# Norm chains whose VectorE steps keep an operand in PSUM, with the adaLN sums held back meanwhile

## The chip, the cores and the metric

The kernel runs on one core of a Trainium2 chip. The metric is the device time of one execution in microseconds (us). TensorE multiplies matrices into PSUM; VectorE, ScalarE and GpSimd work on what lies in SBUF, and the first two of these also on PSUM; SyncE queues the loads. In the profile they are PE (and PEld for its weight loads), DVE, ACT, POOL and SP.

## The reference, cut to what matters

Two layers of a diffusion backbone over 256 latent tokens (`x`) and 256 context tokens (`h`), width 1024. Each sub-layer is preceded by an RMS norm and an adaLN modulation, whose shifts, scales and gates come from a conditioning vector through a large matrix:

```python
def rms_norm(x, g):
    y = xf * lax.rsqrt(jnp.mean(xf * xf, axis=-1, keepdims=True) + RMS_EPS)
    return (y * g).astype(x.dtype)

def modulate(h, shift, scale):
    return h * (1.0 + scale) + shift

for l in range(DEPTH):                       # DEPTH = 2
    sh1, sc1, g1, ..., g3 = split(s_c @ w_mod[l] + b_mod[l], 9)      # and again for the context
    x = x + 0.5 * g1 * swiglu(modulate(rms_norm(x, norm_g[l, 0]), sh1, sc1), ...)
    y, yc = token_mixer(modulate(rms_norm(x, norm_g[l, 1]), sh2, sc2), ...)
    x = x + g2 * y
    x = x + 0.5 * g3 * swiglu(modulate(rms_norm(x, norm_g[l, 2]), sh3, sc3), ...)
```

The context tokens go through the same steps, except that nothing is computed for them behind the mixer of the last layer.

## The kernel before, in words

**Layout.** Activations lie feature-major: `x[k]`, k = 0 to 7, is a tile of 128 features by 512 tokens, of which columns 0 to 255 are the latent tokens (r = 0) and 256 to 511 the context tokens (r = 1). Every fp32 product is made from three TensorE passes over operands split into a rounded part and a rest (`mm3`): `u_hi`, `u_lo` for activations, `w_hi`, `w_lo` for weights. For each weight chunk of 128x1024, ScalarE makes `w_hi` (a cast) and GpSimd makes `w_lo = w_raw - w_hi`, three chunks deep (`SPLIT_BUFS`).

**A norm.** `norm_chain(l, i, r, n)` is a generator for one norm and one half r of the tokens. TensorE sums squares into a PSUM tile `n_ss` (columns 256 and 257). `rsqrt` turns the two sums into 1/sqrt with a bit trick and three Newton rounds, 13 small VectorE steps on the SBUF tiles `rs_v`, `rs_s`, `rs_y`, `rs_a`. `norm_diag` spreads the result over a diagonal matrix `n_diag`, and a matmul with `ones` broadcasts it into columns 0 to 255 of `n_ss`. Then for each k, on 128x256: `n_t = x[k] * A * n_ss` (A is the gain with the adaLN scale), `u_hi = n_t + shift`, `u_lo = n_t + shift - u_hi`. `n_t` is a fresh SBUF tile for each k, and the three steps of successive k are interleaved (n_t of k, u_hi of k-1, u_lo of k-2). With both halves (n > LAT) chain 0 stops after k = 3 until chain 1 has made its first four.

Nine such chains run: both halves for the norms called here (0,1) [layer 0, before the mixer], (0,2) [layer 0, before the second FFN], (1,0) and (1,1), and one for (1,2). The first norm of all, (0,0), has code of its own (`first_tokens`).

**Around it.** A two-half norm is started while TensorE ends the product in front of it (`rest` in `last_down`, or `last_fn`), and is used by `up(..., both=True)` or `proj_f2`: TensorE goes through k = 0 to 3 of r = 0, then of r = 1, with two weight chunks at once, and then through k = 4 to 7 of both with the next two chunks. The second of these needs a weight buffer that the first pass gives back.

**adaLN sums.** Most of the adaLN products are made on VectorE: `mod_gen` adds up `mod_acc = mod_w * scv + mod_acc` over 128x512 tiles, paced at 42 us for two blocks (`MOD_PACE`), as the side "mods". A few blocks are left for TensorE as work within the norms (`norm_fill`, tiles `mod`, `mod_ev`, `mod_t`).

**What sets the order.** Each engine runs its instructions in the order in which the program writes them. `Program.round` resumes all generators in turn (norms, urgent work, sides) after each group of matmuls, and a gated operation is written when a model clock says that its operands are there. A change of any step therefore moves later instructions too. In the profile L196 is the line of all gated operations and L169 of all others, so groups are told apart by their tiles.

Of the kernel before, what the change touches and what calls it, by code (L numbers as in the profile page):

```python
# [11 lines left out]
F32 = mybir.dt.float32  # L12
F32R = mybir.dt.float32r
I32 = mybir.dt.int32
AF = mybir.ActivationFunctionType
ALU = mybir.AluOpType
AX = mybir.AxisListType

P = 128
D = 1024  # L20
KT = D // P
LAT = 256
# [8 lines left out]
EPS = 1e-6  # L31
# [169 lines left out]
class Program:  # L201
# [127 lines left out]
    def round(self):  # L329
        self.wakes = []  # L330
        n = self.clock.count
        self.first = True
        for waiting in (self.norms, self.urgent):
            for g in list(waiting):
                if not self._resume(g):
                    waiting.remove(g)
        self.first = False
        for name in sorted(self.sides, key=lambda name: name == "mods"):
            if name in self.sides:
                self._step(name)  # L340
        return self.clock.count > n
# [91 lines left out]
def tile_backbone(ctx: ExitStack, tc: tile.TileContext, I: dict, out: bass.AP):  # L433
# [4 lines left out]
    sml = ctx.enter_context(tc.tile_pool(name="sml", bufs=4))  # L438
# [7 lines left out]
    prog = Program(nc, rpool, wpool)  # L446
# [3 lines left out]
    gpe, gdve, gact = Gated(prog, "PE", nc.tensor), Gated(prog, "DVE", nc.vector), Gated(prog, "ACT", nc.scalar)  # L450
# [3 lines left out]
    def S(name):  # L454
        return slot.tile([P, 512], F32, name=name, tag="s")
# [60 lines left out]
        yield from gact.copy(r32(hi), src)  # L516
        yield from gdve.tensor_tensor(r32(lo), src, hi, op=ALU.subtract)

    def rsqrt(src, n, scale):

        v = sml.tile([P, 32], F32, name="rs_v", tag="rs_v")[:, :n]
        s = sml.tile([P, 32], F32, name="rs_s", tag="rs_s")[:, :n]
        y = sml.tile([P, 32], F32, name="rs_y", tag="rs_y")[:, :n]
        a = sml.tile([P, 32], F32, name="rs_a", tag="rs_a")[:, :n]
        yield from gdve.tensor_scalar(v, src, scale, EPS, op0=ALU.mult, op1=ALU.add)
        yield from gdve.tensor_scalar(s.bitcast(I32), v.bitcast(I32), 1, None, op0=ALU.logical_shift_right)
        yield from gdve.tensor_scalar(y.bitcast(I32), s.bitcast(I32), -1, 0x5F3759DF, op0=ALU.mult, op1=ALU.add)
        yield from gdve.tensor_scalar(v, v, -0.5, None, op0=ALU.mult)
        for _ in range(3):
            yield from gdve.tensor_tensor(a, y, y, op=ALU.mult)  # L530
            yield from gdve.tensor_tensor(a, a, v, op=ALU.mult)
            yield from gdve.scalar_tensor_tensor(y, a, 1.5, y, op0=ALU.add, op1=ALU.mult)
        return y


    ident = cst.tile([P, P], F32, name="ident")
# [9 lines left out]
    x = [cst.tile([P, NT], F32, name=f"x{k}") for k in range(KT)]  # L546
    scv = cst.tile([P, KT, 32], F32, name="scv")

    st = {"gated": set(), "th": {}}
# [238 lines left out]
    def norm_chain(l, i, r, n):  # L788

        mod = st["mod", l]  # L790
        w = slice(r * LAT, (r + 1) * LAT)
        if r == 0:
            st["A"] = prog.now(norm_scale(l, i, 0, KT))
            st["u"] = [(r32(U("u_hi")), r32(U("u_lo"))) for _ in range(KT)]
            st["done"] = [0, 0]
        yield from prog.banks(1)
        ps = side_bank("n_ss")
        qs = st["sq"]
        for t in range(2):
            c = slice((2 * r + t) * P, (2 * r + t + 1) * P)  # L800
            for j, q in enumerate(qs):
                yield from gmm(ps[:, 256 + t : 257 + t], q[:, c], ones[:, 0:1], j == 0, j == len(qs) - 1)
        rstd = yield from rsqrt(ps[:, 256:258], 2, 1.0 / D)
        dg = yield from norm_diag(rstd, LAT)
        rb = ps[:, :LAT]
        yield from gmm(rb, ones, dg, True, True)
        B = mod[:, 24 * i : 24 * i + 8, :]
        ts = {}
        for step in range(KT + 2):
            k = step  # L810
            if k < KT:
                ts[k] = S("n_t")[:, :LAT]
                yield from gdve.scalar_tensor_tensor(ts[k], x[k][:, w], st["A"][:, k, r : r + 1], rb, op0=ALU.mult, op1=ALU.mult)
            if step == KT - 1:
                prog.release(1)
            k = step - 1
            if 0 <= k < KT:
                hi = st["u"][k][0][:, w]
                yield from gdve.tensor_scalar(hi, ts[k], B[:, k, r : r + 1], None, op0=ALU.add)
            k = step - 2  # L820
            if k >= 0:
                hi, lo = (a[:, w] for a in st["u"][k])
                yield from gdve.scalar_tensor_tensor(lo, ts.pop(k), B[:, k, r : r + 1], hi.bitcast(F32), op0=ALU.add, op1=ALU.subtract)
                st["done"][r] = k + 1
            while r == 0 and n > LAT and k == 3 and st["done"][1] < 4:
                yield None

    def norm_start(l, i, r, n):
        prog.norms.append(norm_chain(l, i, r, n))
# [37 lines left out]
    def norm_diag(rstd, n):  # L867
        nt = n // P
        dg = S("n_diag")[:, :n]
        for t in range(nt):  # L870
            yield from gdve.tensor_scalar(dg[:, t * P : (t + 1) * P], ident, rstd[:, t : t + 1], None, op0=ALU.mult)
        return dg
# [1144 lines left out]
    for l in range(DEPTH):  # L2017
        last = l == DEPTH - 1
        n = LAT if last else NT
# [51 lines left out]
```

## Time and profile before

| | us |
|---|---|
| median of 3 runs | 2881.67 |
| lowest, highest | 2880.91, 2881.89 |
| the profiled execution | 2878.06 |
| its span | 2876.3 |
| TensorE busy in the span | 2777.6 |
| VectorE busy | 1662.6 |
| GpSimd busy | 1288.1 |
| ScalarE busy | 1007.2 |

The span is the time between the first and the last recorded instruction; what is outside it is 1.8 us. An engine counts as busy while an instruction is recorded on it, also while that instruction is held up.

### The profile page before, as it was taken

The numbers are of one execution on the slowest core, as the hardware profiler recorded it, in microseconds if no ns is written. First come the engines' busy times: TensorE is split into PE (matmuls) and PEld (weight loads), VectorE is DVE, ScalarE is ACT, GpSimd is POOL, SyncE is SP. The second block draws the span as 40 slices with busy tenths as digits, with TensorE's granted clock in tenths as the row PEclk, the third lists the DMA queues.
The fourth block names the chain that finished last, engine by engine and source line by source line (L and its number), as shares of the span: only waits on it lengthen the run. The fifth ranks groups of instructions, "written<-read, shape, count | busy, mean of one in ns | idle before, by whom it ended". The sixth has DMA issues, their size and how long they took to land.

```text
span 2876.3 us, 39661 instructions
## 1 busy us (share of the span) xinstructions
PE 2777.6 (97%) x15547; PEld 2330.8 (81%) x15547; DVE 1662.6 (58%) x2970; ACT 1007.2 (35%) x1598; POOL 1288.1 (45%) x585
## 2 busy tenths in 40 slices
PE   8999998999999999999999989999999998999999
PEld 6888877778777888877888878888787777899899
DVE  5654566768765675675545575212555659757522
ACT  2222223433444344322312212222244345454443
POOL 3444433224333442434444434444433455657687
PEclk9999999999999999999999989999999999999999
DMA  6444443224222222433444434333323334435554
GB/s 228 159 147 133 151 129 107 77 81 131 80 73 78 81 74 62 161 125 109 144 143 139 161 102 146 101 96 99 110 70 85 95 100 115 132 103 180 172 184 155
DMA packets 295647, 346.46 MB, mean 120 GB/s; under 512 B 15541, under 2 KB 238806, under 8 KB 295460
## 3 DMA queue, kind: packets, MB, share of 16 engines
q1 hardware_dynamic: 294964, 343.58, 38.0%
q8 instruction: 122, 2.00, 0.3%
q14 instruction: 65, 0.53, 0.1%
q0 software_dynamic: 320, 0.28, 0.0%
q10 hardware_dynamic: 176, 0.07, 0.0%
HBM read 342.83 MB, written 1.05 MB: 120 GB/s over the span
## 4 chain that ended last, share of the span: by engine, by line
PE 86%; DVE 8%; issue 4%; POOL 1%; DMA 0%; ACT 0%; SPq 0%; DVEq 0%; POOLq 0%; ACTq 0%
PE up L169 28%; PE pf L169 17%; PE dn L169 15%; PE pt L169 15%; PE a_s L196 2%; PE a_t L196 2%; PE n_o L196 1%; POOL w_lo L196 1%; PE g_o L196 1%; PE q_o L196 1%; PE g_U L196 1%; PE a_qk L196 1%; DVE rs_a L196 1%; DVE z L169 1%; DVE a_p L196 1%
## 5 line engine op out<-in xcount | busy, mean ns | idle before, releaser
L196 POOL TENSOR_TENSOR w_lo<-w_raw,w_hi 128x1024 fp32r<-128x1024 f32 (+1 forms) x508 | 1228.2, 2422 | 1538.3 <-ACT w_hi L196 1480.3
L196 ACT CAST w_hi<-w_raw 128x1024 fp32r<-128x1024 f32 (+1 forms) x504 | 520.6, 1036 | 993.5 <-issue 311.9
L169 PE MATMUL up<-u_hi,w_lo 128*128 128x512 f32 (+1 forms) x1504 | 534.3, 355 | 16.1 <-POOL w_lo L196 16.0
L169 PE MATMUL up<-u_hi,w_hi 128*128 128x512 f32 (+1 forms) x1504 | 536.5, 357 | 6.4 <-DVE u_hi L196 4.1
L169 PE MATMUL up<-u_lo,w_hi 128*128 128x512 f32 (+1 forms) x1504 | 534.3, 355 | 5.0 <-DVE u_lo L196 4.8
L196 DVE SCALAR_TENSOR_TENSOR mod_acc<-mod_w,scv,mod_acc 128x512 f32<-128x512 f32 x364 | 372.7, 1070 | 57.3 <-DMA mod_w<-w_mod 57.0
L169 PE MATMUL dn<-ff_h,w_hi 128*128 128x512 f32 (+1 forms) x1528 | 396.8, 349 | 0.0
L169 PEld LDWEIGHTS up<-u_hi,w_hi 128*128 128x128 f32 x1504 | 290.9, 193 | 56.0 <-issue 11.0
L169 PEld LDWEIGHTS up<-u_hi,w_lo 128*128 128x128 f32 x1504 | 290.9, 193 | 54.9 <-POOL w_lo L196 17.1
L169 PEld LDWEIGHTS up<-u_lo,w_hi 128*128 128x128 f32 x1504 | 290.7, 193 | 43.4 <-DVE u_lo L196 6.0
L169 PEld LDWEIGHTS dn<-ff_h,w_hi 128*128 128x128 f32 x1528 | 267.6, 189 | 38.9 <-ACT w_hi L196 1.7
L169 PE MATMUL dn<-ff_h,w_lo 128*128 128x512 f32 (+1 forms) x764 | 265.9, 348 | 0.0
L169 PE MATMUL pt<-w_hi,u_hi 128*128 128x512 f32 x640 | 261.8, 409 | 0.0
L169 PE MATMUL pf<-u_hi,w_hi 128*128 128x256 f32 (+1 forms) x736 | 250.9, 341 | 10.3 <-DVE u_hi L196 7.0
L169 PE MATMUL pt<-w_hi,u_lo 128*128 128x512 f32 x640 | 250.8, 392 | 0.0
L169 PE MATMUL pt<-w_lo,u_hi 128*128 128x512 f32 x640 | 250.5, 391 | 0.0
L169 PE MATMUL pf<-u_hi,w_lo 128*128 128x256 f32 (+1 forms) x736 | 239.9, 326 | 8.7 <-POOL w_lo L196 8.7
L169 PE MATMUL pf<-u_lo,w_hi 128*128 128x256 f32 (+1 forms) x736 | 240.3, 327 | 5.8 <-DVE u_lo L196 5.7
L169 DVE TENSOR_TENSOR ff_h<-ff_a,up 128x512 f32<-128x512 f32 (+1 forms) x88 | 53.3, 620 | 317.0 <-PE up L169 278.7
L169 PE MATMUL pf<-y,w_hi 128*128 128x512 f32 (+1 forms) x768 | 195.6, 345 | 3.1 <-DVE y L196 1.9
L169 PEld LDWEIGHTS pf<-u_hi,w_hi 128*128 128x128 f32 x736 | 143.7, 195 | 30.9 <-issue 9.4
L169 DVE SCALAR_TENSOR_TENSOR x<-dn,ff_g,x 128x256 f32<-128x256 f32 x112 | 47.1, 478 | 202.0 <-PE dn L169 201.8
(227 smaller groups left out, 4043.0 us busy)
## 6 DMA issues: line engine op xcount, KB each, us to landing
w_raw<-ffn_w_in SPq DMA_DIRECT2D x176, 512.0 KB
w_raw<-w_in SPq DMA_DIRECT2D x168, 512.0 KB
mod_w<-w_mod SPq DMA_DIRECT2D x288, 256.0 KB
w_raw<-ffn_w_out SPq DMA_DIRECT2D x80, 512.0 KB
w_raw<-w_branch SPq DMA_DIRECT2D x48, 512.0 KB
w_raw<-w_out SPq DMA_DIRECT2D x16, 512.0 KB
w_raw<-ffn_w_out SPq DMA_DIRECT2D x16, 256.0 KB
n_rel<-nat_rpb SPq DMA_DIRECT2D x32, 109.5 KB
```

The costliest lines, as they stand in the source:

```text
L169: return real(*args, **kw)
L196: return real(*args, **kw)
```

## The change

`rsqrt` takes a `room` in PSUM: the norm chains pass columns 258 to 263 of `n_ss`, in which three of its four variables then lie. The Newton step is reordered so that each VectorE step takes one variable from PSUM and at most one from SBUF (`a = y*v`, `a = y*a` in place of `a = y*y`, `a = a*v`). `n_diag` is made by one instruction in place of two. `n_t` is no longer an SBUF tile: it lies in columns 256 to 511 of `n_ss`, one place for all k, and the steps run strictly one after another for each k. The bank is given back at the end of the chain and not after the last `n_t`. And `Program.round` skips the side "mods" while any norm chain is alive, unless the program is waiting for "mods" itself.

```diff
         for name in sorted(self.sides, key=lambda name: name == "mods"):
+            if name == "mods" and self.norms and self.hurry != "mods":
+                continue
             if name in self.sides:
                 self._step(name)
...
-    def rsqrt(src, n, scale):
+    def rsqrt(src, n, scale, room=None):
...
+        w = v
+        if room is not None:
+            w, s, y = (room[:, i * n : (i + 1) * n] for i in range(3))
...
-            yield from gdve.tensor_tensor(a, y, y, op=ALU.mult)
-            yield from gdve.tensor_tensor(a, a, v, op=ALU.mult)
+            yield from gdve.tensor_tensor(a, y, v, op=ALU.mult)
+            yield from gdve.tensor_tensor(a, y, a, op=ALU.mult)
             yield from gdve.scalar_tensor_tensor(y, a, 1.5, y, op0=ALU.add, op1=ALU.mult)
...
-        rstd = yield from rsqrt(ps[:, 256:258], 2, 1.0 / D)
-        dg = yield from norm_diag(rstd, LAT)
+        rstd = yield from rsqrt(ps[:, 256:258], 2, 1.0 / D, ps[:, 258:264])
+        dg = S("n_diag")[:, :LAT]
+        yield from gdve.tensor_tensor(
+            dg.rearrange("p (t c) -> p t c", t=2),
+            ident.unsqueeze(1).broadcast_to([P, 2, P]),
+            rstd.unsqueeze(2).broadcast_to([P, 2, P]),
+            op=ALU.mult,
+        )
...
+        nt = ps[:, LAT:]
+        for k in range(KT):
+            hi, lo = (a[:, w] for a in st["u"][k])
+            b = B[:, k, r : r + 1]
+            yield from gdve.scalar_tensor_tensor(nt, x[k][:, w], st["A"][:, k, r : r + 1], rb, op0=ALU.mult, op1=ALU.mult)
+            yield from gdve.tensor_scalar(hi, nt, b, None, op0=ALU.add)
+            yield from gdve.scalar_tensor_tensor(lo, nt, b, hi.bitcast(F32), op0=ALU.add, op1=ALU.subtract)
+            st["done"][r] = k + 1
             while r == 0 and n > LAT and k == 3 and st["done"][1] < 4:
                 yield None
+        prog.release(1)
```

Three places show how the instructions stand. The first is VectorE in the norm (0,2), chain 0, from the last Newton round on; `x_98` and `x_99` are x[6] and x[7], whose update for the other half of the tokens is queued here. Before:

```order
L196 TENSOR_TENSOR rs_a<-rs_y 128x2
L196 SCALAR_TENSOR_TENSOR mod_acc<-mod_w,scv,mod_acc 128x512 x2
L196 TENSOR_TENSOR rs_a<-rs_a,rs_v 128x2
L196 SCALAR_TENSOR_TENSOR rs_y<-rs_a,rs_y 128x2
L196 TENSOR_SCALAR n_diag<-ident,rs_y 128x128 x2
```

and now:

```order
L196 TENSOR_TENSOR rs_a<-n_ss,rs_v 128x2
L196 TENSOR_TENSOR rs_a<-n_ss,rs_a 128x2
L196 SCALAR_TENSOR_TENSOR n_ss<-rs_a,n_ss 128x2
L196 TENSOR_TENSOR n_diag<-ident,n_ss 128x256
L169 SCALAR_TENSOR_TENSOR x_98<-pf,mx_g,x_98 128x256
L169 SCALAR_TENSOR_TENSOR x_99<-pf,mx_g,x_99 128x256
L196 SCALAR_TENSOR_TENSOR n_ss<-x_92,n_A,n_ss 128x256
L196 TENSOR_SCALAR u_hi<-n_ss,mod_312 128x256
L196 SCALAR_TENSOR_TENSOR u_lo<-n_ss,mod_312,u_hi 128x256
```

The adaLN sums are gone from the chain, the diagonal stands ahead of the two updates and not behind the third Newton round that followed them, and the three steps of one k stand in a row.

The second is the end of the same norm on VectorE, where the SwiGLU product `ff_h` of the FFN comes next. Before:

```order
L196 TENSOR_SCALAR u_hi<-n_t,mod_312 128x256
L196 SCALAR_TENSOR_TENSOR u_lo<-n_t,mod_312,u_hi 128x256 x3
L196 TENSOR_SCALAR mod_acc<-mod_w,scv 128x512 x2
L196 SCALAR_TENSOR_TENSOR mod_acc<-mod_w,scv,mod_acc 128x512 x4
L169 TENSOR_TENSOR ff_h<-ff_a,up 128x512 x2
```

and now:

```order
L196 SCALAR_TENSOR_TENSOR n_ss<-x_99,n_A,n_ss 128x256
L196 TENSOR_SCALAR u_hi<-n_ss,mod_312 128x256
L196 SCALAR_TENSOR_TENSOR u_lo<-n_ss,mod_312,u_hi 128x256
L196 SCALAR_TENSOR_TENSOR mod_acc<-mod_w,scv,mod_acc 128x512 x2
L169 TENSOR_TENSOR ff_h<-ff_a,up 128x512 x2
```

The held-back sums follow right behind the last `u_lo`, two of them ahead of `ff_h`.

The third is TensorE in the norm (0,1), from the end of the FFN's last product on; `mod<-mod_w` are the blocks that TensorE fills in, `n_ss<-ones` the sums of squares of chain 1. Before:

```order
L169 MATMUL mod<-mod_w,scv 32x512 x4
L196 MATMUL n_ss<-ones,sq_sum 128x1
L196 MATMUL n_ss<-ones,sq 128x1 x2
...
L196 MATMUL n_ss<-n_diag,ones 128x256
L196 MATMUL mod_t<-ident,mod_ev 128x128 x4
L169 MATMUL pf<-u_hi,w_hi 128x256
```

and now:

```order
L196 MATMUL n_ss<-n_diag,ones 128x256
L169 MATMUL mod<-mod_w,scv 32x512 x4
L196 MATMUL n_ss<-ones,sq_sum 128x1
L196 MATMUL n_ss<-ones,sq 128x1 x2
...
L169 MATMUL pf<-u_hi,w_hi 128x256
```

The broadcast of chain 0 moved ahead of the filled-in block and of chain 1's sums.

## Rows read from the trace of the kernel before

**Rows 1.** The page, busy time of the engines: share of the span, instructions.

```profile
PE 2777.6 (97%) x15547; PEld 2330.8 (81%) x15547; DVE 1662.6 (58%) x2970; ACT 1007.2 (35%) x1598; POOL 1288.1 (45%) x585
```

**Rows 2.** Stretches around the five norms: length, TensorE busy (instructions), granted clock, DMA.

```profile
395.00:452.00 57.00, 45.60 (x325) 0.88 0.29 89
1262.00:1320.00 58.00, 44.14 (x296) 0.79 0.25 82
1660.00:1715.00 55.00, 43.23 (x297) 0.84 0.26 86
2052.00:2105.00 53.00, 46.30 (x309) 0.97 0.28 77
2660.00:2700.00 40.00, 35.90 (x270) 1.00 0.49 157
```

**Rows 3.** Every stretch near half clock in those norms, same columns; nine, one shown, summed.

```profile
1292.50:1295.90 3.40, 3.40 (x18) 0.57 0.01 2
...
sum 58.20, PE 38.42; mean PE 4.27
```

**Rows 4.** The same product at either clock, same columns.

```profile
415.80:418.80 3.00, 3.00 (x16) 0.50 0.07 18
419.30:422.80 3.50, 3.50 (x31) 1.00 0.02 5
```

**Rows 5.** Waits of TensorE in 1262:1320, norm (0,2): us, times, longest.

```profile
PE up L169 <- POOL w_lo L196: 6.8, 1, 6.8
PE n_ss L196 <- DVE n_diag L196: 4.2, 1, 4.2
```

**Rows 6.** Waits of TensorE in 380:460, norm (0,1).

```profile
PE pf L169 <- DVE u_hi L196: 5.1, 2, 4.6
PE pf L169 <- POOL w_lo L196: 4.8, 1, 4.8
```

**Rows 7.** Waits of TensorE in 1660:1715, norm (1,0).

```profile
PE up L169 <- POOL w_lo L196: 6.3, 1, 6.3
```

**Rows 8.** Waits of TensorE in 2035:2115, norm (1,1).

```profile
PE pf L169 <- DVE u_lo L196: 4.4, 4, 2.4
```

**Rows 9.** VectorE in the norm (0,2): start, us, operation.

```profile
1271.39 0.16 DVE L196 TENSOR_TENSOR rs_a<-rs_a,rs_v 128x2 f32<-128x2 f32 x1
1271.59 0.16 DVE L196 SCALAR_TENSOR_TENSOR rs_y<-rs_a,rs_y 128x2 f32<-128x2 f32 x1
...
1273.19 2.31 DVE L196 TENSOR_TENSOR rs_a<-rs_a,rs_v 128x2 f32<-128x2 f32 x1
1275.53 2.26 DVE L196 SCALAR_TENSOR_TENSOR rs_y<-rs_a,rs_y 128x2 f32<-128x2 f32 x1
```

**Rows 10.** GpSimd in the same norm, with the idle time before and its releaser.

```profile
1272.75 5.02 POOL L196 TENSOR_TENSOR w_lo<-w_raw,w_hi 128x1024 fp32r<-128x1024 f32 x2 [11.48 <-ACT w_hi L196]
1300.19 9.62 POOL L196 TENSOR_TENSOR w_lo<-w_raw,w_hi 128x1024 fp32r<-128x1024 f32 x2 [22.41 <-ACT w_hi L196]
```

**Rows 11.** The chain's steps over the execution: ns min/median/max, first and last start, forms.

```profile
L196 DVE SCALAR_TENSOR_TENSOR n_t<-x,n_A,n_ss x72: 468/476/482, 413.0 to 2681.5; 128x256 f32<-128x256 f32 x72
L196 DVE TENSOR_SCALAR u_hi<-n_t,mod x72: 339/348/2370, 413.9 to 2682.5; 128x256 fp32r<-128x256 f32 x72
L196 DVE SCALAR_TENSOR_TENSOR u_lo<-n_t,mod,u_hi x72: 467/480/2590, 414.9 to 2683.2; 128x256 fp32r<-128x256 f32 x72
```

**Rows 12.** VectorE in the norm (0,2), two successive k.

```profile
1292.29 0.48 DVE L196 SCALAR_TENSOR_TENSOR n_t<-x,n_A,n_ss 128x256 f32<-128x256 f32 x1
...
1293.34 0.48 DVE L196 SCALAR_TENSOR_TENSOR n_t<-x,n_A,n_ss 128x256 f32<-128x256 f32 x1
```

**Rows 13.** VectorE in the second mixer, a step and the next, which takes its result.

```profile
2617.15 0.42 DVE L169 SCALAR_TENSOR_TENSOR m_w<-m_t,pf 128x256 f32<-128x256 f32 x1 [0.97 <-PE pf L169]
2617.61 0.42 DVE L169 TENSOR_TENSOR z<-z,m_w 128x256 f32<-128x256 f32 x1
```

**Rows 14.** A one-input VectorE step from PSUM into SBUF: busy us, mean ns, idle before.

```profile
L196 DVE COPY y<-n_o 128x256 f32<-128x256 f32 x8 | 3.4, 423 | 11.1 <-PE n_o L196 11.1
```

More of the change, by code (lines that the diff above doesn't have):

```diff
@@ L517, in split_to @@
         yield from gdve.tensor_tensor(r32(lo), src, hi, op=ALU.subtract)
-    def rsqrt(src, n, scale):
[L521 to L526, printed above, removed]
+    def rsqrt(src, n, scale, room=None):
+        v, s, y, a = (sml.tile([P, 32], F32, name=f"rs_{x}", tag=f"rs_{x}")[:, :n] for x in "vsya")
+        w = v
+        if room is not None:
+            w, s, y = (room[:, i * n : (i + 1) * n] for i in range(3))
+        yield from gdve.tensor_scalar(w, src, scale, EPS, op0=ALU.mult, op1=ALU.add)
+        yield from gdve.tensor_scalar(s.bitcast(I32), w.bitcast(I32), 1, None, op0=ALU.logical_shift_right)
         yield from gdve.tensor_scalar(y.bitcast(I32), s.bitcast(I32), -1, 0x5F3759DF, op0=ALU.mult, op1=ALU.add)
-        yield from gdve.tensor_scalar(v, v, -0.5, None, op0=ALU.mult)
+        yield from gdve.tensor_scalar(v, w, -0.5, None, op0=ALU.mult)
         for _ in range(3):
-            yield from gdve.tensor_tensor(a, y, y, op=ALU.mult)
-            yield from gdve.tensor_tensor(a, a, v, op=ALU.mult)
+            yield from gdve.tensor_tensor(a, y, v, op=ALU.mult)
+            yield from gdve.tensor_tensor(a, y, a, op=ALU.mult)
             yield from gdve.scalar_tensor_tensor(y, a, 1.5, y, op0=ALU.add, op1=ALU.mult)
@@ L807, in norm_chain @@
         B = mod[:, 24 * i : 24 * i + 8, :]
[L808 to L824, printed above, removed]
+        nt = ps[:, LAT:]
[6 more added lines that the diff above has]
+            st["done"][r] = k + 1
             while r == 0 and n > LAT and k == 3 and st["done"][1] < 4:
                 yield None
+        prog.release(1)
     def norm_start(l, i, r, n):
```

## The prediction, as it was put on record

> **What bounds the kernel now.** First the page: TensorE is busy for 2777.6 of 2876.3 us [rows 1], so the time is TensorE's, and a change of VectorE work can only give back what TensorE loses in waits or in a lowered clock. Next I looked at the norms, the only places that the diff touches, and read the table of stretches around the five that it changes [rows 2]. Length less busy time is TensorE's idle time: 11.4, 13.9, 11.8, 6.7 and 4.1 us, together 47.9 us. In the first four the granted clock is below 1 as well. Nine stretches in them stand at the lower of TensorE's two levels (1.2 GHz; their means read a little over half because the cuts at the edges are not exact), and TensorE is busy in them for 38.42 us [rows 3]. The same product takes 3.00/16 = 0.188 us per matmul there and 3.50/31 = 0.113 us at full clock [rows 4], so 40% of that busy time, 15.3 us, is lost. All in all the norms cost 63 us; no more can be won.
>
> The waits say who is late: GpSimd's `w_lo` for 6.8, 4.8 and 6.3 us in the norms (0,2), (0,1) and (1,0) [rows 5 to 7], and VectorE's chain: 4.2 us for the diagonal, 5.1 us for `u_hi`, 4.4 us for `u_lo` [rows 5, 6, 8]. Both have one cause. A Newton step of 0.16 us takes 2.31 us and ends at 1275.50, the next takes 2.26 us and ends at 1277.79 [rows 9]; two GpSimd splits run from 1272.75 to 1277.77 [rows 10], so each step is held until a split ends. The other way round, two splits that took 5.02 us there take 9.62 us from 1300.19 on, while VectorE runs the last `u_lo` and then `mod_acc`; with the second at its usual 2.5, the first takes 7.1 us. Which steps are hit is what matters. `n_t`, with one tensor in SBUF and one in PSUM, was never held in 72 instances (maximum 482 ns); `u_hi` and `u_lo`, with all tensors in SBUF, reach 2370 and 2590 ns [rows 11]. After the change every step of a chain takes at most one tensor from SBUF and one from PSUM, like `n_t`.
>
> **The change part by part.** *Newton steps and diagonal.* Thirteen dependent small steps, one start every 0.20 us [rows 9], are 2.6 us as before. No row shows a VectorE result in PSUM; I take the SBUF step for it, and bound the difference under rival B. The diagonal becomes one step that I take at `n_t`'s 0.48 us [rows 11]. What goes are the held steps and the `mod_acc` steps between them: in (0,2) the two holds are 4.3 us, and the diagonal behind them was what TensorE waited for, 4.2 us. With the diagonal earlier, the broadcast moves ahead of TensorE's filled-in block, which then covers the first k; the first wait of each norm goes to 0.
>
> *The three steps of each k.* Before, interleaved, one k took 1293.34 - 1292.29 = 1.05 us [rows 12]. Now each step waits for the one before. Such a pair starts 2617.61 - 2617.15 = 0.46 us apart where the first takes 0.42 [rows 13], so a dependence costs 0.04 us beyond the duration. `u_hi` now reads PSUM: 0.42 us, as the copy of that size [rows 14], for 0.35. One k is 0.48 + 0.42 + 0.48 + 3 x 0.04 = 1.50 us. TensorE takes twelve matmuls per k, 12 x 0.113 = 1.35 us. So VectorE falls from ahead of TensorE to just behind it: 0.15 us lost on each of 8 k in a row (four of each chain), 1.2 us per norm. The last eight k run beside each other and beside TensorE's wait for `w_lo`; I put them at nothing, and at another 1.2 us per norm if that cover is gone.
>
> For `u_hi` there is a rule against the change. The Trainium skill, page "VectorE: DVE Perf Modes", section "Why PSUM operands drop a tier", says that an fp32 step with a PSUM operand loses the mode of two elements per cycle; the rows agree, 0.35 us against 0.42. By it 72 instances cost 5 us of VectorE, nearly all of it beside TensorE; by the rows it is what stands in the 1.50 us.
>
> *`w_lo`.* In (0,2) the split falls from 7.1 to 2.5 us, and TensorE's wait with it from 6.8 to 2.2 us. The split can start only when the first pass frees a weight buffer, so this much stays. I take 2.2 us for (0,1) and (1,0) too.
>
> *What else stays in each of the first three norms.* Chain 1's first `u_hi` and `u_lo` behind its broadcast: 0.52 + 0.46 + 0.52 = 1.5 us. One stretch at the lower clock behind the wait for `w_lo`: as the 3.40 us in [rows 3], 40% of it, 1.4 us; 0 if the short wait does not lower the clock. With 2.2 and 1.2 that is 6.3 us per norm.
>
> *Fourth and fifth norm.* In (1,1), the context's half feeds one product and not two, so TensorE needs 0.68 us per k there and VectorE's 1.50 shows: 4 x (1.50 - 1.05) = 1.8 us more than before. The waits for `u_lo` (4.4 us) go, one for `w_lo` (2.2 us), so far covered by them, appears. The balance, 0.4, rises by part of the 1.4 us of its one slow stretch; I take 1 us gained, bounds -2 and 4. In (1,2) the clock is full and the idle time 4.1 us [rows 2], which bounds the gain; eight k at 0.15 bound the loss, 1.2. I take 0.
>
> *adaLN sums.* Those that stood between a chain's steps, some ten per norm in the first three, now come behind it. Each is at most twice an `n_t`, as it has twice the columns: 9.5 us of VectorE per norm, moved into stages in which VectorE is busy for 58% on average [rows 1]. The order moves their groups 100 to 300 matmuls back, and nowhere piles them up ahead of the place that needs them. I take 1 us lost; 0 if hidden, 9.5 if a third of the three portions shows.
>
> *Sum, against the profiled span of 2876.3 us.* Norms one to three: idle 11.4 + 13.9 + 11.8 = 37.1 us; lower clock 15.3 less the fourth norm's 1.4 = 13.9; together 51.0, of which 3 x 6.3 = 18.9 stay: 32.1 gained. Plus 1, less 1: 32.1. Span 2844.2, execution 2846.0 with the 1.8 us outside it. The median of the runs is 3.6 us above the profiled execution, so the median goes from 2881.67 to 2849.6. I put 2850.
>
> **The rivals.**
> *A, half the gain.* The wait for `w_lo` keeps its length, because the sums held back come right behind the chain and hold GpSimd in its place. Then 17.9 - 6.6 = 11.3 us of wait stay, and with the longer idle times one more slow stretch per norm (3 x 1.4): 32.1 - 15.5 = 16.6 gained, 2865. For it: the order is made by a model clock that knows nothing of holds. Against it: when the buffer is freed, VectorE still has eight k ahead of it, 8 to 12 us at 1.05 to 1.50, and the split needs 2.5.
>
> *B, slower: the serial chain becomes the bound.* On TensorE's way lie 8 k in each of four norms and 8 in the fifth, 40 in all. The gain of 32 us is used up when one k takes 32/40 = 0.8 us more, 2.3 us in all, which is 0.27 us for each of three dependences beyond the 0.04. At 0.41 beyond it the kernel takes 40 x 1.23 - 32 = 17 us more, 2899. For it: a result that goes through PSUM has no row, and each k is now a strict row of three. Against it: `n_t` reads PSUM without delay, and a dependence costs only 0.04 us where it is seen. The Trainium skill, same page, section "Rules for kernel authors", speaks for B: it advises to copy out of PSUM first if many steps follow. The trace has no chain that would show it.
>
> *C, no change.* The waits in the norms go, but a later one ends last: TensorE arrives some 10 us earlier at each norm's end, and if the next weights or the stage behind were late by as much, the time would stay within 5 us, about 2879. Against it: TensorE is busy for 97% of the span, so few waits exist to absorb it.
>
> **How the numbers follow.** The forecast, 2850, with its own range 2833 to 2861: 0.60. The lower end takes the slow stretches (4.2), the fourth and fifth norm's upper bounds (7) and 6 us of chance in the reordering elsewhere; the upper end the shown sums (8.5) and some of the same chance. A: 0.22, 2858 to 2873. C: 0.08. B: 0.10. The range that holds 8 in 10 is 2831 to 2872. A measurement of this kernel can tell about 0.2%, 6 us, from no change; faster by more than that: 0.60 + 0.22 = 0.82; within it 0.08; slower 0.10.
>
> **What would show it.** Right: idle times of 6 us or less in the stretches of the first three norms and a granted clock of 0.9 or more; no step of a chain above 0.6 us; the split behind the first pass at 2.5 us and TensorE's wait for it near 2.2; successive `n_t` of one chain 1.5 us apart. Wrong: successive `n_t` over 2.3 us apart (B); that split still above 5 us (A); short idle times in the norms but new ones in the stages behind (C); or a lower clock that stays although the idle times went.

## The result, and the profile after

The changed kernel takes 2836.01 us (median of four runs, 2833.64 to 2838.28) against 2881.29 us for the kernel before in the same comparison: a ratio of 0.9845, 95% interval 0.9828 to 0.9862, or 45 us less. The forecast was 2850, with 2833 to 2861 as its own range and 2831 to 2872 as the range that holds 8 in 10: the direction is right and the time lies in both, but 14 us below the forecast and near the lower end. One of the four executions of e7, below, ran at a lower granted clock (0.906) and took 2921.95 us; the median given for e7 is that of the other three. The profiled execution took 2838.28 us, its span is 2836.5, 39.8 us shorter than before.

The page of after, busy time of the engines (for [rows 1]):

```profile
PE 2768.3 (98%) x15547; PEld 2318.7 (82%) x15547; DVE 1669.1 (59%) x2960; ACT 1008.7 (36%) x1599; POOL 1282.0 (45%) x585
```

VectorE is as busy as before (1669 us, 1663 before), and the number of matmuls is the same. The 40 us are TensorE's: 9 us less busy time, 30 us less idle time. To see where, the execution is cut into stages that begin and end at the same matmul in every kernel here: a norm's stage runs from the first sum of squares to the end of the 96th matmul of `pt` behind it (mixer) or the 672nd of `up` (FFN). Table of stretches of the kernel before: length, TensorE busy (instructions), granted clock, DMA share and rate; in this order the norm (0,1), the rest of the first mixer, the norms (0,2), (1,0), (1,1), and the rest of the second mixer:

```profile
398.07:473.16 75.09, 63.69 (x393) 0.91 0.31 95
473.16:1264.20 791.04, 785.32 (x4244) 1.00 0.31 93
1264.20:1431.46 167.26, 153.40 (x777) 0.93 0.36 120
1661.29:1830.79 169.50, 155.59 (x789) 0.94 0.34 114
2054.86:2115.82 60.96, 54.26 (x333) 0.97 0.27 75
2115.82:2666.54 550.72, 525.91 (x3440) 0.98 0.38 113
```

The same stages of after:

```profile
398.49:463.25 64.76, 61.46 (x393) 0.97 0.32 96
463.25:1260.71 797.46, 789.01 (x4244) 1.00 0.31 94
1260.71:1411.13 150.42, 147.21 (x777) 1.00 0.37 119
1640.31:1791.41 151.10, 148.25 (x777) 0.99 0.38 123
2017.17:2075.99 58.82, 55.02 (x333) 0.97 0.27 77
2075.99:2626.91 550.92, 526.10 (x3441) 0.98 0.38 113
```

The first three norms are 10.3, 16.8 and 18.4 us shorter, together 45.6; twelve matmuls have moved from (1,0) into the FFN behind it, which is 1.7 us longer for that, so 43.9 net. (1,1) gives 2.1 more. The first mixer gives 6.4 us back. The rest changes by less than 1 us in any stage. Length less busy time is idle time: 11.4, 13.9, 13.9 and 6.7 us in the four norms before, 3.3, 3.2, 2.9 and 3.8 now; and the clock went from 0.91 to 0.97, 0.93 to 1.00 and 0.94 to 0.99.

TensorE's waits in after, in 1260:1300 (norm (0,2)) and then in 1640:1680 (norm (1,0)): us in total, times, longest; they answer to [rows 5, 7]:

```profile
PE up L169 <- DVE u_lo L196: 1.4, 2, 0.9
PE up L169 <- DVE u_hi L196: 1.1, 1, 1.1
PE up L169 <- POOL w_lo L196: 0.3, 1, 0.3
...
PE up L169 <- POOL w_lo L196: 0.9, 1, 0.9
PE up L169 <- DVE u_lo L196: 0.8, 2, 0.6
PE up L169 <- DVE u_hi L196: 0.7, 1, 0.7
```

The waits of 6.8 and 6.3 us for `w_lo` have shrunk to 0.3 and 0.9 us, and the one of 4.2 us for the diagonal is gone. The chain's steps over the whole execution (ns minimum/median/maximum; for [rows 11]):

```profile
L196 DVE SCALAR_TENSOR_TENSOR n_ss<-x,n_A,n_ss x72: 481/490/491, 405.8 to 2646.6; 128x256 f32<-128x256 f32 x72
L196 DVE TENSOR_SCALAR u_hi<-n_ss,mod x72: 475/484/486, 406.3 to 2647.1; 128x256 fp32r<-128x256 f32 x72
L196 DVE SCALAR_TENSOR_TENSOR u_lo<-n_ss,mod,u_hi x72: 474/484/486, 406.8 to 2647.7; 128x256 fp32r<-128x256 f32 x72
L196 DVE SCALAR_TENSOR_TENSOR n_ss<-rs_a,n_ss x27: 155/165/166, 402.1 to 2630.8; 128x2 f32<-128x2 f32 x27
L196 DVE TENSOR_TENSOR n_diag<-ident,n_ss x9: 410/421/423, 403.5 to 2631.0; 128x256 f32<-128x256 f32 x9
```

The maxima are what to read: none of these steps is more than 3 ns above its median, where `u_hi` and `u_lo` reached 2370 and 2590 ns before. VectorE in the norm (0,2), one k and the start of the next (for [rows 12]: start, us, operation), and GpSimd's splits behind the first pass (for [rows 10]):

```profile
1268.90 0.49 DVE L196 SCALAR_TENSOR_TENSOR n_ss<-x,n_A,n_ss 128x256 f32<-128x256 f32 x1 [1.10 <-PE n_ss L196]
1269.43 0.48 DVE L196 TENSOR_SCALAR u_hi<-n_ss,mod 128x256 fp32r<-128x256 f32 x1
1269.95 0.49 DVE L196 SCALAR_TENSOR_TENSOR u_lo<-n_ss,mod,u_hi 128x256 fp32r<-128x256 f32 x1
1270.47 0.49 DVE L196 SCALAR_TENSOR_TENSOR n_ss<-x,n_A,n_ss 128x256 f32<-128x256 f32 x1
...
1286.21 4.73 POOL L196 TENSOR_TENSOR w_lo<-w_raw,w_hi 128x1024 fp32r<-128x1024 f32 x2 [12.22 <-ACT w_hi L196]
```

One k takes 1270.47 - 1268.90 = 1.57 us (1.05 before), and the two splits take 4.73 us in place of 9.62.

### The profile page after: what moved, and what is told of

Read it like the earlier page. It is cut to its first block, busy times and chain, and to the rows that moved or that the text cites. A ratio compares the mean times of both kernels' runs of the same rounds, so it can differ in the third digit from the quotient of the medians.

```text
span 2836.5 us, 39679 instructions
## 1 busy us (share of the span) xinstructions
PE 2768.3 (98%) x15547; PEld 2318.7 (82%) x15547; DVE 1669.1 (59%) x2960; ACT 1008.7 (36%) x1599; POOL 1282.0 (45%) x585
## 3 DMA queue, kind: packets, MB, share of 16 engines
HBM read 342.83 MB, written 1.05 MB: 121 GB/s over the span
## 4 chain that ended last, share of the span: by engine, by line
PE 87%; DVE 8%; issue 3%; POOL 1%; DMA 0%; ACT 0%; SPq 0%; DVEq 0%; POOLq 0%; ACTq 0%
PE up L169 29%; PE pf L169 18%; PE dn L169 15%; PE pt L169 13%; PE a_s L196 2%; PE a_t L196 2%; PE n_o L196 1%; PE g_o L196 1%; PE q_o L196 1%; PE g_U L196 1%; DVE a_p L196 1%; PE a_qk L196 1%; POOL w_lo L196 1%; DVE rs_y L196 1%; DVE z L169 1%
## 5 line engine op out<-in xcount | busy, mean ns | idle before, releaser
L196 DVE SCALAR_TENSOR_TENSOR mod_acc<-mod_w,scv,mod_acc 128x512 f32<-128x512 f32 x364 | 371.7, 1069 | 58.9 <-DMA mod_w<-w_mod 58.8
L169 PEld LDWEIGHTS dn<-ff_h,w_lo 128*128 128x128 f32 x764 | 144.6, 189 | 18.4
```

Of the source, the lines that this page charges most:

```text
L169: return real(*args, **kw)
L196: return real(*args, **kw)
```

## The experiments

The theory, P: VectorE's steps on SBUF operands and GpSimd's splits hold each other up, and the place of the operands ends that. Its rivals: S, the adaLN sums in VectorE's queue were what delayed the chains; O, the new order of the steps. Lengths in us; the median of the kernel before was 2880.6 beside the first four, 2882.1 beside the next four, 2881.7 beside the last three. The row of the changed kernel comes from its first runs.

| kernel | median | (0,1) | first mixer | (0,2) | (1,0) | (1,1) | second mixer |
|---|---|---|---|---|---|---|---|
| before | 2881.3 | 75.1 | 791.0 | 167.3 | 169.5 | 61.0 | 550.7 |
| changed | 2836.0 | 64.8 | 797.5 | 150.4 | 151.1 | 58.8 | 550.9 |
| stand-back alone (e1) | 2868.6 | 79.4 | 790.7 | 161.9 | 159.5 | 58.9 | 551.7 |
| PSUM alone (e2) | 2850.0 | 67.1 | 792.4 | 159.5 | 161.3 | 58.8 | 551.0 |
| `n_t` back in SBUF (e3) | 2868.4 | 79.8 | 788.0 | 161.4 | 159.6 | 63.0 | 553.0 |
| Newton back in SBUF (e4) | 2841.6 | 65.4 | 794.8 | 151.2 | 155.3 | 59.8 | 554.2 |
| same order, all in SBUF (e5) | 2865.6 | 72.2 | 794.3 | 158.2 | 158.8 | 64.7 | 554.0 |
| q and k norms in PSUM too (e6) | 2832.7 | 64.4 | 793.9 | 150.4 | 149.8 | 58.8 | 553.0 |
| two places for `n_t` (e7) | 2835.8 | 65.0 | 795.8 | 150.7 | 152.5 | 55.5 | 551.1 |
| sums paced at 40 us (e8) | 2837.6 | 64.1 | 795.8 | 150.4 | 150.3 | 58.8 | 553.5 |
| e6 and e7 (e9) | 2829.8 | 65.0 | 792.7 | 152.2 | 149.5 | 55.5 | 551.2 |
| e6 and the softmax in PSUM (e10) | 2834.3 | 64.4 | 794.5 | 150.4 | 151.1 | 58.8 | 553.2 |
| changed, again (e11) | 2834.4 | 64.8 | 794.2 | 150.4 | 151.1 | 58.8 | 550.2 |

### The two halves of the change alone (e1, e2)

e1 is the kernel before with this alone; e2 is the changed kernel without it.

```diff
         for name in sorted(self.sides, key=lambda name: name == "mods"):
+            if name == "mods" and self.norms and self.hurry != "mods":
+                continue
```

> The kernel before with one part of the change alone: the adaLN sums stand back while a norm is under way; the chain's operands stay in SBUF. Theory P (the place of the operands): VectorE's steps on SBUF operands and GpSimd's splits still hold each other up, so Newton steps of 2.3 us and splits of 5 to 7 us remain in the norms, and the gain is a third of the 45 us or less: 2866 to 2881. Theory S (the sums): what delayed the chains were the sums between and behind their steps, so this part alone brings most of the gain: 2836 to 2850, and the split behind the first pass of each norm takes about 2.5 us.

Measured: 2868.61 us, ratio 0.9951 (0.9936 to 0.9966), 12 us gained. GpSimd, then VectorE, then TensorE's wait in the norm (0,2) of e1:

```profile
1301.17 8.83 POOL L196 TENSOR_TENSOR w_lo<-w_raw,w_hi 128x1024 fp32r<-128x1024 f32 x2 [19.39 <-ACT w_hi L196]
...
1302.73 2.73 DVE L196 SCALAR_TENSOR_TENSOR mod_acc<-mod_w,scv,mod_acc 128x512 f32<-128x512 f32 x4
...
PE up L169 <- POOL w_lo L196: 6.0, 1, 6.0
```

With the second split at its usual 2.4 us, the first takes 6.5 us though no sum stands between the chain's steps: first the last `u_lo`, then the held-back sums, four in a row right behind the chain, keep GpSimd waiting. In (0,1) the split takes 8.0 us, and that stage is even 4.3 us longer than before. That is rival A of the prediction, as it is without PSUM.

> The changed kernel without the stand-back of the sums: operands of the chain in PSUM, the sums between its steps as before. Theory P: no step of a chain is held, only the sums' own 0.7 us lie between them, and two thirds or more of the gain stay: 2836 to 2852. Theory S: 2865 to 2881, since the sums still stand between the steps and still hold GpSimd's split.

Measured: 2850.04 us, ratio 0.9893 (0.9877 to 0.9910), 31 us gained, as P expected. No step of a chain is held and the splits take 2.4 to 2.8 us, but 14 us are missing to the whole change. Waits of TensorE in the norm (0,2) of e2, and VectorE there:

```profile
PE up L169 <- DVE u_lo L196: 5.7, 7, 2.4
PE up L169 <- DVE u_hi L196: 1.9, 3, 0.9
...
1285.21 0.49 DVE L196 SCALAR_TENSOR_TENSOR n_ss<-x,n_A,n_ss 128x256 f32<-128x256 f32 x1
1285.61 1.59 DVE L196 SCALAR_TENSOR_TENSOR mod_acc<-mod_w,scv,mod_acc 128x512 f32<-128x512 f32 x1
1287.12 0.47 DVE L196 SCALAR_TENSOR_TENSOR u_lo<-n_ss,mod,u_hi 128x256 fp32r<-128x256 f32 x1
```

In the first 45 us of that norm 18 sums are queued between the chain's steps (4 in the changed kernel), and TensorE waits 7.6 us for `u_hi` and `u_lo` (2.5 in the changed kernel). So S holds for a part: the sums cost their own time in the queue (0.74 us each as a rule), and two of these 18 were held besides (1.59 and 1.02 us). 12 and 31 us alone, 45 together: the halves add up to within 3 us, less than the 4.6 by which the changed kernel's own runs differ.

### One part undone (e3, e4)

e3 puts `n_t` back into SBUF, interleaved as before; Newton steps, diagonal and stand-back stay:

```diff
-        nt = ps[:, LAT:]
-        for k in range(KT):
...
+        ts = {}
+        for step in range(KT + 2):
+            k = step
+            if k < KT:
+                ts[k] = S("n_t")[:, :LAT]
...
```

> The changed kernel with n_t back in SBUF and its three steps interleaved as before; Newton steps and diagonal keep their PSUM operands, the sums stand back. Theory P: u_hi and u_lo read and write SBUF alone again, are held by splits or hold them; the split behind the first pass of a norm takes 5 us or more and TensorE waits 3 us or more for it in the first three norms: 2848 to 2862. Theory S: the place of n_t is of no matter, and one k in 1.05 us in place of 1.57 even helps: 2830 to 2840.

Measured: 2868.39 us, ratio 0.9953 (0.9938 to 0.9968): no better than the stand-back alone, a little above P's 2848 to 2862. The split is slow again, 6.5 us and then 2.4, and TensorE's wait for it is 6.0 us as in e1. GpSimd in its norm (0,2):

```profile
1295.98 8.83 POOL L196 TENSOR_TENSOR w_lo<-w_raw,w_hi 128x1024 fp32r<-128x1024 f32 x2 [18.93 <-ACT w_hi L196]
```

So of the PSUM half nearly everything (32 us) hangs on `n_t`: on its place or on the row of its steps, which e3 changes together and e5 tells apart. e4 is the changed kernel with the Newton variables and the two-step diagonal as before:

```diff
-        rstd = yield from rsqrt(ps[:, 256:258], 2, 1.0 / D, ps[:, 258:264])
+        rstd = yield from rsqrt(ps[:, 256:258], 2, 1.0 / D)
...
+        dg = yield from norm_diag(rstd, LAT)
```

> The changed kernel with the Newton steps and the diagonal as before (SBUF variables, diagonal in two steps); n_t in PSUM, the sums stand back. Theory P: where a split runs beside the Newton steps, one or two of them are held for 2.3 us each, in two or three of the norms, and TensorE waits for the diagonal again: 2842 to 2856. Theory S: no difference from the changed kernel, 2833 to 2840.

Measured: 2841.63 us, ratio 0.9861 (0.9847 to 0.9876), 5.6 us more than the changed kernel and just below P's lower end. The intervals of the two ratios overlap, but each of its four runs (2840.16 to 2843.08) is above each of the changed kernel's eight (2832.60 to 2838.28). VectorE in its norm (1,0), and TensorE's wait there:

```profile
1645.88 1.75 DVE L196 TENSOR_SCALAR rs_s<-rs_v 128x2 int32<-128x2 int32 x1
1647.67 2.27 DVE L196 TENSOR_SCALAR rs_y<-rs_s 128x2 int32<-128x2 int32 x1
...
PE up L169 <- DVE u_hi L196: 4.2, 1, 4.2
```

Two held steps of 0.17 us cost 3.7 us, and TensorE waits 4.2 us for the first `u_hi` behind them; that stage is 4.2 us longer than in the changed kernel.

### Place or order (e5)

```diff
-        rstd = yield from rsqrt(ps[:, 256:258], 2, 1.0 / D, ps[:, 258:264])
+        rstd = yield from rsqrt(ps[:, 256:258], 2, 1.0 / D)
...
-        nt = ps[:, LAT:]
         for k in range(KT):
...
+            nt = S("n_t")[:, :LAT]
```

> The changed kernel with the same steps in the same strict order (n_t, u_hi, u_lo of one k in a row, one step for the diagonal, the reordered Newton step, the sums standing back), but with n_t and the Newton variables in SBUF tiles. Theory P (place): splits and steps hold each other again, the split behind the first pass of a norm takes 5 us or more: 2860 to 2876, as the run with n_t interleaved in SBUF (2868) gave. Theory O (order): the gain of the PSUM part came from the new order of the steps and the earlier broadcast, and 2836 to 2846 remains.

Measured: 2865.59 us, ratio 0.9941 (0.9926 to 0.9956): O falls, the order alone keeps little more than the stand-back gives. But one expectation of P failed too. GpSimd, VectorE and a wait in the norm (0,2) of e5:

```profile
1294.79 4.73 POOL L196 TENSOR_TENSOR w_lo<-w_raw,w_hi 128x1024 fp32r<-128x1024 f32 x2 [17.36 <-ACT w_hi L196]
...
1295.29 4.38 DVE L196 TENSOR_SCALAR u_hi<-n_t,mod 128x256 fp32r<-128x256 f32 x2
...
PE up L169 <- DVE u_lo L196: 4.5, 3, 2.1
```

The splits are as short as in the changed kernel (2.4 us), and it is VectorE that is held: two `u_hi` take 4.38 us. In e3, also with `n_t` in SBUF, GpSimd was held at that place: VectorE's sums end at 1300.29 there and the split at 1302.48, 2.2 us later. That e3 interleaves its steps is not the whole difference, for an earlier split of e3's norm (0,2) meets interleaved steps as well. GpSimd's two splits there, and VectorE:

```profile
1272.34 4.71 POOL L196 TENSOR_TENSOR w_lo<-w_raw,w_hi 128x1024 fp32r<-128x1024 f32 x2 [11.48 <-ACT w_hi L196]
...
1272.77 2.08 DVE L196 TENSOR_SCALAR u_hi<-n_t,mod 128x256 fp32r<-128x256 f32 x1
```

These splits start beside an `n_t` and a held `u_hi` and have their usual length, and it is `u_hi` that is held. What the rows show is this: in the norms of before, e1 and e3 ten splits take 5.3 to 8.0 us, and behind the start of each of them only `u_hi`, `u_lo` and adaLN steps follow one another in VectorE's row, without a gap and without another `n_t`. In e5's strict order an `n_t` stands ahead of every `u_hi`, up to the last k, and none of its splits in the norms takes more than 2.9 us. No run varies this alone, so how the two engines take turns stays open. One of the two pays either way.

### What is left: the strict row, and the first mixer (e6 to e11)

e7 gives each chain a second bank, so that `n_t` has two places and successive k can be interleaved:

```diff
-        yield from prog.banks(1)
+        yield from prog.banks(2)
         ps = side_bank("n_ss")
+        tt = side_bank("n_tt")
...
+        yield from n_t(0)
+        for k in range(KT):
...
+            yield from gdve.tensor_scalar(hi, nt[k % 2], b, None, op0=ALU.add)
+            if k + 1 < KT:
+                yield from n_t(k + 1)
+            yield from gdve.scalar_tensor_tensor(lo, nt[k % 2], b, hi.bitcast(F32), op0=ALU.add, op1=ALU.subtract)
```

> The changed kernel with a second PSUM bank per chain, so that n_t has two places and the three steps of successive k can be interleaved: u_hi of k, n_t of k+1, u_lo of k. In the changed kernel dependent steps start 0.52 us apart and one k takes 1.57 us; independent steps of the kernel before started 0.39 us apart, so one k should take 3 x 0.39 = 1.18 us, under TensorE's 1.35. If the strict row of steps costs what was left in the norms (8.6 us of waits for u_hi and u_lo in four norms), 2 to 7 us are gained: 2829 to 2835. If those waits belong to each chain's first steps, or the second bank is waited for, nothing is gained or up to 8 us lost: 2835 to 2844.

Measured: 2835.80 us, ratio 0.9840 (0.9820 to 0.9860): no difference to the changed kernel in the whole. VectorE in its norm (0,2), `u_hi` of one k and of the next, and TensorE's waits there:

```profile
1273.81 0.48 DVE L196 TENSOR_SCALAR u_hi<-n_ss,mod 128x256 fp32r<-128x256 f32 x1
...
1274.99 0.48 DVE L196 TENSOR_SCALAR u_hi<-n_tt,mod 128x256 fp32r<-128x256 f32 x1
...
PE up L169 <- POOL w_lo L196: 1.8, 1, 1.8
PE up L169 <- DVE u_hi L196: 1.1, 1, 1.1
PE up L169 <- DVE u_lo L196: 0.4, 1, 0.4
```

One k takes 1.18 us, as expected, and yet the waits of that norm add up to 3.3 us against 2.8. What was saved at `u_lo` (1.4 to 0.4) came back at `w_lo` (0.3 to 1.8): TensorE reaches the next weight earlier and waits there for a split that starts hardly sooner (25.0 us after the norm's beginning, 25.5 in the changed kernel). Only in (1,1) did the faster row help: 55.5 us against 58.8 in six executions with the strict row (changed, e2, e6, e8, e10, e11).

e8 changes only the pace of the sums (`MOD_PACE` 42.0 to 40.0), e11 changes nothing.

> The changed kernel with the adaLN sums paced at 40 us for two blocks in place of 42, so that their places in the order shift everywhere and nothing else is changed. It shows how much a mere shift of the order moves the time: within 5 us of the changed kernel, 2831 to 2841, if the first mixer's loss of 6 us is a matter of where its steps happen to meet GpSimd's splits, with that mixer's length changed by 2 us or more; the same loss in the first mixer again, to 1 us, if it follows from the earlier arrival of TensorE.

> The changed kernel once more, on the same chip as the two others, so that differences of 3 us can be read: 2834 to 2839.

e8: 2837.55 us, ratio 0.9844 (0.9824 to 0.9864); e11: 2834.35, ratio 0.9836 (0.9822 to 0.9849). In e8 the first mixer is 1.7 us shorter than in the changed kernel's first profiled execution, between the two outcomes expected, so its parts have to be read. In all three executions TensorE waits 1.6 us for `q_rot` in the first mixer, which it never did before, and its idle time there is 8.4 us (5.7 before). VectorE in the changed kernel's first mixer, and that wait:

```profile
951.47 2.38 DVE L196 SCALAR_TENSOR_TENSOR rs_y<-rs_a,rs_y 128x8 f32<-128x8 f32 x1
...
957.03 2.68 DVE L196 TENSOR_TENSOR q_sw<-q_raw,cossin 128x128 f32<-128x128 f32 x2
...
PE a_qk L196 <- DVE q_rot L196: 1.6, 1, 1.6
```

So 2.7 us of the 6.4 that were given back are idle time, behind steps of other norms that splits hold. How much earlier TensorE arrives is not what counts: e5 begins this mixer only 3.3 us earlier than the kernel before, the changed kernel 9.9, and e5 has the same wait of 1.6 us and the same 8.4 us of idle time. Steps of these norms were held before, too (a `q_rot<-q_raw,cossin` at 958.95 for 2.6 us), but TensorE did not wait for them: which steps meet a split has changed. Another part is the clock. The first mixer of e11, the same program as the changed kernel:

```profile
461.56:1255.78 794.22, 785.84 (x4243) 1.00 0.31 94
```

It is 3.2 us shorter than in the first profiled execution, with the same idle time: two stretches of 3.4 us at the lower clock do not occur. So a stretch costs 1.6 us here, and e7 and e8, with one stretch each, lie between (795.8 us). The kernel before has one as well (granted clock 0.50 from 501.1 to 504.5): one more of them is 1.6 of the remaining 3.7 us, and some 2 us of longer TensorE busy time stay open. The norms of the two executions agree to 0.03 us.

e6 gives the norms of q and k the same remedy:

```diff
+        yield from prog.banks(1)
+        room = side_bank("h_rs")
-        rstd = yield from rsqrt(ss[:, : nt * nb], nt * nb, 1.0 / hd)
+        rstd = yield from rsqrt(ss[:, : nt * nb], nt * nb, 1.0 / hd, room[:, : 3 * nt * nb])
...
+        prog.release(1)
```

> The changed kernel with the same remedy in the mixers' norms of q and k: their Newton variables and their result lie in a PSUM bank that is taken for the time of the norm. In the changed kernel such a step was held for 2.38 us, TensorE then waited 1.6 us for q_rot and stood at the lower clock for 3.4 us. Theory P: these holds go from those norms, and 1 to 5 us of the 6 us that the first mixer gave back return: 2831 to 2837. Rival: the bank is missing elsewhere in the mixers, or another step is late next: 2836 to 2848.

Measured: 2832.66 us, ratio 0.9827 (0.9813 to 0.9842). The wait for `q_rot` is gone, the first mixer's idle time is 5.9 us again and its length 793.9, 3.6 us below the changed kernel's first profiled execution, with 6.8 us at the lower clock in both. In the medians the difference, 1.7 to 3.4 us against the changed kernel's two sets of runs, is not clear of the noise. e9 has e6 and e7 together:

> The changed kernel with both additions: the q and k norms' Newton variables in PSUM, and two places for n_t. If both effects seen before add up (3.6 us in the first mixer by the one, 3.3 us in the norm (1,1) by the other): 2828 to 2833. If the second bank of each chain takes back what the one gains, or differences of 3 us are only shifts of the order: 2833 to 2840.

Measured: 2829.75 us (2828.12 to 2833.81), ratio 0.9821 (0.9808 to 0.9835), beside 2834.35 (2832.60 to 2836.26) for the changed kernel on the same chip: some 5 us less. In the profiled executions the first mixer (idle 5.9 us) is 1.5 us shorter and (1,1) (55.5 us) 3.3, and other stages take back a part (the span is 2.0 us shorter). The intervals of the two ratios overlap, so it is the likely best, not a proven one. e10 takes the idea to the softmax:

```diff
-                    p[it][:, s], sc[it][:, s], AF.Exp, bias=mx[it][:, b : b + 1], accum_out=sm[it][:, b : b + 1]
+                    sc[it][:, s], sc[it][:, s], AF.Exp, bias=mx[it][:, b : b + 1], accum_out=sm[it][:, b : b + 1]
...
-                yield from gdve.tensor_scalar(p[it][:, s], p[it][:, s], rs[:, b : b + 1], None, op0=ALU.mult)
+                yield from gdve.tensor_scalar(p[it][:, s], sc[it][:, s], rs[:, b : b + 1], None, op0=ALU.mult)
```

> The changed kernel with the q and k norms' Newton variables in PSUM and, beyond that, the softmax: the exponentials stay in the PSUM bank of the scores, and VectorE's scaling reads them from there, right behind them, into SBUF. In the changed kernel this scaling is held in 33 of 144 instances, 42.7 us together, and TensorE waits 6.0 us for it. Theory P: no such step is held any more; 2 to 8 us are gained over the run with the q and k norms alone (2833): 2825 to 2831. Rival: each wave of scores keeps its banks one scaling longer, TensorE's wait for banks (8.0 us before) grows by about 0.5 us for each of 36 waves: 2833 to 2850.

Measured: 2834.29 us, ratio 0.9836 (0.9823 to 0.9849): nothing gained over e6. The scaling over the whole execution, in the changed kernel and in e10:

```profile
L196 DVE TENSOR_SCALAR a_p<-a_p,a_rs x144: 340/486/2671, 698.5 to 2566.4; 128x512 f32<-128x512 f32 x96, 128x256 f32<-128x256 f32 x48
...
L196 DVE TENSOR_SCALAR a_p<-a_s,a_rs x144: 469/746/754, 694.2 to 2569.9; 128x512 f32<-128x512 f32 x96, 128x256 f32<-128x256 f32 x48
```

Held instances are gone (754 ns at most), but each 128x512 step is 0.26 us longer. TensorE's wait for the scaled scores rises to 10.5 us (6.0 in the changed kernel, 8.9 in e6); its wait for the scores' banks falls to 2.6 (8.0 in the changed kernel), where the rival had expected it to grow. Together that is 13.1 us, against 14.0 in the changed kernel. The remedy pays where a few steps lie on TensorE's path and meet a split, not wherever steps are held.

## Why the prediction was right, and where it was off

**What bounds the kernel, and the cause.** Right in the main: TensorE's idle time and lower clock in the norms were what could be won, and the held steps and splits were most of it (the changed kernel against e5, which has the same order and another place: 30 us). Too narrow in "both have one cause": the sums in the queue were a second one. They are worth 12 us alone and 14 on top of PSUM (e1, e2); the prediction had only a price for moving them, 1 us lost, and left what their going brings inside the 32 us, without a term of its own.

**Newton steps and diagonal.** Right: 0.20 us per step, no hold, TensorE's waits for the diagonal gone. The diagonal takes 0.42 us (0.48 taken). Together with the reordered steps they are worth 5.6 us (e4).

**The three steps of each k.** 1.57 us for 1.50, from 0.52 us per dependent step three times. The 0.04 us beyond the duration came out; the difference is `u_hi`, which takes 0.48 us and not the 0.42 of the copy. Close in size.

**What stays in each norm: the step that failed.** The prediction added 2.2 us for `w_lo`, 1.2 for the strict row and 1.5 for chain 1's first steps, 4.9 us of idle time per norm, 14.7 in three. Measured are 3.3, 3.2 and 2.9, together 9.4. The split does take the 2.4 us put down for it, but TensorE waits 0.3, 0.3 and 0.9 us for it: while it runs, TensorE is still behind on `u_lo`. These waits lie beside each other, and e7 shows it from the other side: with the strict row taken away the wait for `w_lo` is 1.8 us. The two were added, and had to be taken as the larger of them: 5.3 us too much stayed. The larger alone would have left 3.7 us per norm, so the overlap explains 3.6 of the 5.3; the rest lies mainly in smaller first waits (0.4, 1.1 and 0.7 us for `u_hi`) than the 1.5 taken, less a wait of 1.4 us for `mod_acc` in (0,1), which is among the 9.4.

**The lower clock.** Three stretches of 3.4 us were put down for the first three norms; there are two in the profiled execution (stages (0,1) and (1,0), 0.97 and 0.99), 1.4 us less. The mechanism held in these norms: where the waits went, most of the lower clock went with them. It is not a price per wait: in the first mixer the same 8.4 us of idle time came with two stretches and with none.

**The edge of the window.** The stretch of (1,0) was cut at 1715 us, and something of the same kind lies just behind. TensorE's wait and a stretch at the lower clock in the kernel before:

```profile
PE mod L196 <- DVE mod_acc L196: 2.1, 1, 2.1
...
1726.00:1729.40 3.40, 3.40 (x15) 0.57 0.86 317
```

Both are gone there in after: 2.1 us and 40% of 3.4, another 3.5 us that no term held. 5.3, 1.4 and 3.5 are 10.2 of the 11.8 us by which the first three norms' net gain (43.9) is above the 32.1; the remaining 1.6 us, by difference, is TensorE busy time, perhaps lower clock before that was priced too low; no run separates it.

**Fourth and fifth norm.** (1,1) gained 2.1 us (1 taken, bounds -2 and 4), (1,2) 0.2 (0 taken). That the strict row shows in (1,1) was right, and its price was too small: 3.3 us by e7, 1.8 taken. The slow stretch there costs nothing of its own now: with the strict row the stage lasts 58.8 us at a granted clock of 0.94 (e8), 0.97 (changed) and 1.00 (e2) alike, so VectorE's row sets its length.

**The sums moved.** They show in one wait, 1.4 us for `mod_acc` in (0,1), where there was none before; 1 us was taken. In the stages behind the norms they do not show. What the prediction didn't see is that the first mixer would give 6.4 us back by another way: other steps of its own norms meet splits (2.7 us of idle time, in the changed kernel, e8 and e11 alike), one more stretch at the lower clock (1.6), and some 2 us that stay open. The prediction had called the norms the only places that the diff touches; the reordered Newton step runs in the mixers' norms of q and k as well, but e4, with the old order everywhere, has the same wait of 1.6 us for `q_rot`. Rival C had named a later wait that absorbs the gain; one came, with 2.7 us where C needed nearly all of it.

**The sum.** 43.9 + 2.1 - 6.4, and the small changes elsewhere, make the 39.8 us of the span; forecast were 32.1. In part that is errors that cancel: the norms gave 12.9 us more than forecast (11.8 and 1.1), and the first mixer took 6.4 that no term held. The rest of the way to the 45 us of the medians is variation between executions: the second profiled execution of the same program has a span of 2830.8 us, 45.5 under before.

**The rivals.** A (the split keeps its length) is what e1 shows without PSUM; in the changed kernel the split ends at 1290.9 and the first sums start at 1295.1, so they don't meet. B (the serial chain bounds) would have needed 2.3 us per k; 1.57 were measured. The Trainium skill, page "VectorE: DVE Perf Modes", section "Rules for kernel authors", gives two ways for elementwise work on a matmul's output, to accept the slower rate from PSUM or to copy to SBUF first when many steps follow; beside a busy GpSimd the runs decide against SBUF, 2868 and 2866 us with `n_t` there against 2836. **The signs** named came out: idle time under 6 us, clock 0.97 or more, no step above 0.6 us, the split at 2.4, successive `n_t` 1.57 us apart; only TensorE's wait near 2.2 us did not.

## What to carry to other kernels

When VectorE's short steps now and then take as long as one GpSimd instruction, look at the operands: keep one of them in PSUM on the chain that TensorE waits for, even if the single step gets longer, and keep bulk work out of that queue meanwhile; each alone brought a part. When several waits of one place are priced, ask which of them run beside each other before adding them, and let the window reach past the last one. Expect that a changed order brings other steps beside the splits, and read the stages that the change doesn't touch, too.

## What the runs showed of the hardware

All from the rows of this case. What is held is told by the operands: in the changed kernel none of the chains' 216 steps on `n_t`, `u_hi` and `u_lo` and none of the 136 residual updates `x<-dn,ff_g,x` and `x<-pf,mx_g,x`, all with a tensor in PSUM and at most one input from SBUF, is more than 11 ns above its median, while `a_p<-a_p,a_rs`, with one tensor from SBUF into SBUF, is held (more than 0.3 us above the median) in 33 of 144 instances and `mod_acc`, with two, in 69 of 364 (up to 2.9 us). A `TENSOR_REDUCE` with its only tensor in SBUF (`h_ss<-h_sq`, 48 instances) has a maximum of 686 ns at a median of 676. This fits the Trainium skill, page "SBUF — State Buffer", section "Who interferes with whom", by which a VectorE instruction with at most one SBUF input contends with GpSimd only in the modes that use two ports, and one with two SBUF inputs contends with a GpSimd instruction that reads SBUF.

Who pays was not expected: a row of `u_hi`, `u_lo` and adaLN steps without a gap and without an `n_t` keeps a split of 2.4 us waiting until it takes 5.3 to 8.0 us (ten splits of before, e1 and e3); where an `n_t` runs or is still to come, the split has its usual length, and `u_hi` or `u_lo` is held, to 1.9 to 2.5 us a time in e5. Why the engines take turns in this way is not shown.

Dependent steps on 128x256 with an operand in PSUM start 0.52 us apart (0.49 long, changed kernel), independent ones 0.39 apart with the same length (e7): steps that don't wait overlap by 0.09 us, so a strict row costs 0.13 us a step and not only the 0.04 us beyond the duration.
